# Dilated mixer: tokens sorted by class, half of one group's transposes on VectorE, operands at 256 bytes, seams' norms on VectorE

## The chip, the cores and the metric

The kernel runs on one core of a Trainium2 chip, as a single launch. The metric is the device time of that launch in microseconds (us), less is better. The engines are called as in the profile: PE is TensorE (matrix multiplies and transposes), PEld its weight loads, DVE is VectorE, ACT is ScalarE, POOL is GpSimd, SP is SyncE, which issues the weights' DMAs.

## The reference

A four-layer encoder works on 512 tokens of 1024 features, batch 1. Each layer is a mixer and a SwiGLU feed-forward part (F), each with a norm before and after and a residual. Layers 0 and 3 have the dilated mixer (A), layer 1 an axial-rope attention (B), layer 2 a latent attention (C). So the stages run A, F, B, F, C, F, A, F. The part that the change is mostly about is the dilated mixer:

```python
A_GROUPS = ((128, 1), (512, 4), (2048, 16))     # window, dilation
...
def mixer_a(x, wqkv, wo):
    qkv = (x @ wqkv).reshape(B, S, 3, A_NG, A_HEADS, A_HEAD_DIM)   # 3 groups, 16 heads of 64
    for g, (window, dilation) in enumerate(A_GROUPS):
        o, l = dilated_window_attention(qkv[:, :, 0, g], qkv[:, :, 1, g], qkv[:, :, 2, g], window, dilation, slopes[g])
    wgt = jax.nn.softmax(jnp.stack(lses, axis=0), axis=0)
    o = jnp.sum(wgt[..., None] * jnp.stack(outs, axis=0), axis=0)
    return o.reshape(B, S, -1) @ wo
```

In a group of dilation d a token attends to the tokens of its own residue mod d within the window, with a bias that is linear in the distance. With 512 tokens, the second group (d = 4) has four residues of 128 tokens each, and the third (d = 16) has sixteen of 32 tokens each.

## The kernel before, in words

**Numbers.** Everything is float32 in and out. A product is made from high and low parts: `split` (L136) rounds a tile to a high part on ACT (L138) and takes the rest on DVE (L139), and `mm3` (L170) issues three matmuls, high with high (L172), high with low (L173), low with high (L174). Weights arrive as `raw` by DMA from SP and are split to `whi`, `wlo`. The normed input of a stage is kept transposed in `yh`, `yl`, and the hidden values of a feed-forward part in `hT`. A trace row names out<-moving,stationary: `psa<-yh,whi` streams 512 columns of yh against a 128x128 block of whi, `psp<-whi,hT` streams whi against a block of hT.

**PSUM.** Banks of 128x512 float32 come in four tags with two buffers each: psa (projections), pss (scores), psp (transposes), pso (values).

**The dilated mixer** goes over eight pairs of heads p. A pair has eight units (hh, bp): hh is the head, bp 0 and 1 are the two halves of the first group's queries, bp 2 and 3 the two halves of the second and third group's. For bp 2 and 3 the 512 tokens stand in four blocks by residue mod 4; in a block's 128x256 tile of scores the columns 0 to 127 are the second group's keys and 128 to 255 the third group's, whose entries outside the residue mod 16 are put far away by the distance table `dist` (t2 in `const_tables`). Per unit: `scores` makes the matmuls, a DVE operation adds the bias and takes the row minimum (L625), ACT exponentiates (L628) into p; `transposes` turns p in four PE transposes 128x128 (L642) into one psp bank, split into pT (L138, L139); `values` multiplies pT with v. There are 64 units a mixer, two mixers in the program, so 128 units and 512 transposes at L642, of which 64 units have bp above 1. Between the units' steps the PE works at a filler, the projections of the next pair, in an order that is written out by hand; the other engines' order is made by a scheduler. At the end of a pair the group's maxima and sums go through HBM (`scr`) back into token order, by one DMA out (L632) and one in (L634), both issued by POOL, and `weigh` and `spread` make the weights of the groups from them. For the last pair `spread_fast` does that with transposes at L735.

**Seams.** At the end of a stage `rows_out` evacuates token tile t = 0 to 3 one after the other, adds to the residual h (L291), and makes the next stage's input with `pre_norm` (L191), whose transposes follow in `norm_t` (L226). `pre_norm` has two forms. The ordinary one multiplies h by the gain on POOL (L201, two operations of 128x512) while ACT sums the squares, and later scales one half on ACT (L209) and one on POOL (L210). The one called fast does both products in two DVE operations (L207) once the factor r is there (POOL, L218); only the first stage of the program uses it.

**Places in SBUF.** In the built program `yh` starts 192 bytes past a multiple of 256 in a partition, and so do `yl`, `raw`, `whi` and `wlo`; the pools of a stage (hT, pT, kd, y, q, kT, cT, wx, v) start 64 past one, and `ident` 128 past one.

Of the kernel before, what the change touches and what calls it, by code (L numbers as in the profile page):

```python
# [10 lines left out]
F32 = mybir.dt.float32  # L11
F32R = mybir.dt.float32r
AF = mybir.ActivationFunctionType
# [24 lines left out]
def const_tables():  # L38

    f = np.float32  # L40
    q = np.arange(P)[:, None]
    w = np.arange(2 * P)[None, :]
    d0 = np.abs(w - 64 - q)
    t0 = np.where(d0 <= 64, d0, BIG).astype(f)
    l = np.arange(P)[None, :]
    d1 = np.abs(l - q)
    t1 = np.where(d1 <= 64, 4.0 * d1, BIG).astype(f)
    t2 = np.where((l - q) % 4 == 0, 4.0 * d1, BIG).astype(f)
    dist = np.concatenate([t0, t1, t2], axis=1)

    def angles(pos, dim):
        half = dim // 2
        fr = np.power(f(10000.0), -np.arange(half, dtype=f) * f(2.0) / f(dim)).astype(f)
        return (pos.astype(f)[:, None] * fr[None, :]).astype(f)

    t = np.arange(S)
    cs, sn = [], []
    for pos in (t // 64, t % 64):
        a = angles(pos, 64)
        c, s = np.cos(a), np.sin(a)  # L60
        cs += [c, c]
        sn += [-s, s]
    bcos = np.concatenate(cs, axis=1).astype(f)
    bsin = np.concatenate(sn, axis=1).astype(f)

    a = angles(t, 32)
    c, s = np.cos(a).astype(f), np.sin(a).astype(f)
    ccos = np.concatenate([c, c], axis=1)
    csin = np.concatenate([-s, s], axis=1)
    sc = f(96.0 ** -0.5)  # L70
    cq = np.empty((P, S), f)
    cq[:64] = -sc
    cq[64:96] = -(ccos.T * sc)
    cq[96:] = -(csin.T * sc)
    return {
        "t_dist": dist,
        "t_bcos": bcos,
        "t_bsin": bsin,
        "t_ckr": np.concatenate([ccos, csin], axis=1),
        "t_cq": cq,  # L80
    }
# [26 lines left out]
class Net:  # L108
    def __init__(self, ctx, tc, a):
        self.tc, self.nc, self.a = tc, tc.nc, a  # L110
        nc = self.nc
        pool = lambda name, bufs, **k: ctx.enter_context(tc.tile_pool(name=name, bufs=bufs, **k))
        self.base = pool("base", 1)
        self.wp = pool("wp", 4)
        self.work = pool("work", 2)

        self.small = pool("small", 6)
        self.ps = pool("ps", 2, space=bass.MemoryType.PSUM)
        self.ident = self.base.tile([P, P], F32, name="ident")
        make_identity(nc, self.ident)  # L120
        self.mhalf = self.base.tile([P, 16], F32, name="mhalf")
        nc.vector.memset(self.mhalf, -0.5)
        self.h = [self.base.tile([P, D], F32, name=f"h{t}") for t in range(NB)]
        self.yh = self.base.tile([P, KD, S + 64], F32R, name="yh")
        self.yl = self.base.tile([P, KD, S + 64], F32R, name="yl")
        self.n = 0
# [120 lines left out]
    def rows_out(self, yp, stat, nf, w, acc_in, final, late=None, R=5):  # L247
# [98 lines left out]
        for t in range(NB):  # L346
            for pr in range(cut, npair):
                if pr == npair - 2 and t >= 2:
                    self.flush(1)
                for f in (2 * pr, 2 * pr + 1):  # L350
                    one(banks[t], f, t, ws[pr])
                yield 1.3
            evac(t, 1, banks[t])
            if "pre" not in gains:
                nc.sync.dma_start(out=self.a["out"][t * P:(t + 1) * P, :], in_=self.h[t])
            else:
                self.pending.append(lambda t=t, yn=self.pre_norm(t, gains["pre"]): self.norm_t(t, yn, final[2]))


    def ffn(self, i, final):  # L360
# [61 lines left out]


    def mixer_a(self, j, final):


        nc, tc = self.nc, self.tc
# [47 lines left out]
        def proj_v12(p):  # L475


            vt = {}

            def turn(g, tag="a"):  # L480
                bk = self.bank(tag)
                for c in range(NB):
                    nc.tensor.transpose(bk[:, c * P:(c + 1) * P], vt[g][:, c * P:(c + 1) * P], self.ident)
                if g == 1:
                    st["v12"] = [new(f"v12{i}", [P, NB, 256]) for i in range(2)]
                t = [x[:, :, (g - 1) * P:g * P] for x in st["v12"]]
                self.split(t[0], t[1], bk.rearrange("p (c e) -> p c e", c=NB))

            for g in (1, 2):
                wt = qk_load(g, 2, p)  # L490
                bk = self.bank("a")
                for k in range(KD):
                    qk_mm(bk, wt, slice(0, S), k)
                    yield 0.65
                    if g == 2 and k == 2:
                        turn(1)
                        yield 0.45
                vt[g] = self.work.tile([P, D], F32, tag="yn", name=self.uid("vt"))[:, :S]
                nc.scalar.activation(vt[g].rearrange("p (r l) -> p r l", r=NB),
                                     bk.rearrange("p (l r) -> p r l", r=NB), AF.Copy)  # L500
                if g == 1:
                    yield from wait(8 * p + 2)

            def rest(tag="a"):
                turn(2, tag)
                done.add(("v12", p))

            st["turn"] = rest
# [14 lines left out]

        lower, upper = slice(0, 64), slice(64, P)

        def lo_scaled(out, src, hi):
            nc.vector.scalar_tensor_tensor(out, src, -0.125, hi.bitcast(F32), op0=ALU.mult, op1=ALU.subtract)

        def qk_evac(bk, g, s):
            for hh in range(2):  # L530
                src = bk[hh * 64:hh * 64 + 64]
                if g == 0 and s == 0:
                    q = st["q", hh] = new(f"q{hh}", [P, S])
                    nc.scalar.activation(q[lower], src, AF.Copy, scale=-0.125)
                    lo_scaled(q[upper], src, q[lower])
                elif g == 0:
                    kh, kl = st["k", hh] = new(f"kh{hh}", [P, S]), new(f"kl{hh}", [P, S])
                    nc.scalar.activation(kh[lower], src, AF.Copy)
                    nc.scalar.activation(kh[upper], src, AF.Copy)
                    nc.vector.tensor_tensor(kl[lower], src, kh[lower].bitcast(F32), op=ALU.subtract)  # L540
                    nc.gpsimd.tensor_copy(kl[upper], kl[lower].bitcast(F32))
                else:
                    rows = (lower, upper)[g - 1]
                    src = src.rearrange("p (l r) -> p r l", r=4)
                    if s == 0:
                        if g == 1:
                            st["y", hh] = [new(f"y{hh}{i}", [P, S]) for i in range(2)]
                        h, l = [x[rows].rearrange("p (r l) -> p r l", r=4) for x in st["y", hh]]
                        nc.scalar.activation(h, src, AF.Copy, scale=-0.125)
                        lo_scaled(l, src, h)  # L550
                    else:
                        self.split(kd[hh][0][rows, :, g - 1, :], kd[hh][1][rows, :, g - 1, :], src)

        def proj_qk(p, g, s, unit):
            wt = qk_load(g, s, p)
# [30 lines left out]
        def scores(p, hh, bp):  # L586
# [42 lines left out]
            st["p", p, hh, bp] = pp  # L629
            if hh == 1 and bp == 3:  # L630
                sc = self.scr[p % 2]
                nc.gpsimd.dma_start(out=sc.rearrange("(l r) c -> l r c", r=4), in_=xs)  # L632
                xn = ap.tile([P, NB, 4], F32, tag="xn", name=self.uid("xn"), bufs=2)
                nc.gpsimd.dma_start(out=xn, in_=sc.rearrange("(b p) c -> p b c", p=P))  # L634
                st["xn", p] = xn

        def transposes(p, hh, bp):
            pp = st.pop(("p", p, hh, bp))
            tp = self.bank("p")
            for i in range(2):  # L640
                for c in range(2):
                    nc.tensor.transpose(tp[:, (2 * i + c) * P:(2 * i + c + 1) * P],  # L642
                                        pp[:, i, c * P:(c + 1) * P], self.ident)
            st["last"] = self.split(pT[0][:, bp % 2], pT[1][:, bp % 2], tp)

        def values(p, hh, bp):
# [33 lines left out]
            if bp == 3:  # L680
                if hh == 0:
                    st["op", p] = new("op", [P, S], F32)
                nc.scalar.activation(st["op", p][rows].rearrange("p (l r) -> p l r", r=4),
                                     out[:64].rearrange("p (r l) -> p l r", r=4), AF.Copy)

        def weigh(p):

# [601 lines left out]
    def run(self, stages):  # L1289
# [43 lines left out]
                self.rest(2)  # L1333
        for n, st in enumerate(stages):
            nxt = stages[n + 1] if n + 1 < len(stages) else None
            final = (post(st), pre(nxt) if nxt else None, bool(nxt) and nxt[0] == "A")
            kind, j, i = st
            run = {"F": self.ffn, "A": self.mixer_a, "B": self.mixer_b, "C": self.mixer_c}[kind]
            with ExitStack() as es:
# [39 lines left out]
```

## Time and profile before

| | |
|---|---|
| time, median of 3 runs | 3064.25 us (3064.14 to 3065.21) |
| profiled execution | 3065.5 us |
| its span | 3063.7 us |
| PE busy | 3026.5 us, 99% |
| PEld, DVE, ACT, POOL busy | 84%, 51%, 46%, 14% |
| mean granted clock of PE | 0.998 of full |

The span runs from the first instruction to the last of one profiled execution; its time has some 2 us around it. Busy is time in which an instruction of the engine was under way. Matmuls are pipelined, so each is recorded longer (389 ns for 512 columns) than the step from one start to the next. Full speed of the clock is 2.4 GHz.

### The profile page before, as it was taken

The numbers are of one execution on the slowest core, as the hardware profiler recorded it, in microseconds if no ns is written. First come the engines' busy times: TensorE is split into PE (matmuls) and PEld (weight loads), VectorE is DVE, ScalarE is ACT, GpSimd is POOL, SyncE is SP. The second block draws the span as 40 slices with busy tenths as digits, with TensorE's granted clock in tenths as the row PEclk, the third lists the DMA queues.
The fourth block names the chain that finished last, engine by engine and source line by source line (L and its number), as shares of the span: only waits on it lengthen the run. The fifth ranks groups of instructions, "written<-read, shape, count | busy, mean of one in ns | idle before, by whom it ended". The sixth has DMA issues, their size and how long they took to land.

```text
span 3063.7 us, 42230 instructions
## 1 busy us (share of the span) xinstructions
PE 3026.5 (99%) x16102; PEld 2568.6 (84%) x16102; DVE 1552.2 (51%) x3120; ACT 1420.5 (46%) x3073; POOL 430.3 (14%) x628
## 2 busy tenths in 40 slices
PE   9999999999999999999999999999999999999998
PEld 8888888888887888888888888888888888888886
DVE  5555556533346863333578633235555555643233
ACT  5555556532234653223478632234555555542232
POOL 1111111300003330000254400003011111210000
PEclk9999999999999999999999999999999999999999
DMA  5222222332332123333211233332322223233332
GB/s 148 76 84 77 83 84 84 108 100 95 97 108 67 56 83 97 100 93 105 75 51 36 90 96 97 96 101 75 90 83 84 79 82 90 84 101 99 91 99 73
DMA packets 286810, 269.11 MB, mean 88 GB/s; under 512 B 9776, under 2 KB 246544, under 8 KB 286608
## 3 DMA queue, kind: packets, MB, share of 16 engines
q1 hardware_dynamic: 280736, 250.84, 27.3%
q0 software_dynamic: 5872, 15.59, 1.8%
q8 instruction: 126, 2.06, 0.3%
q14 instruction: 76, 0.62, 0.1%
HBM read 264.04 MB, written 2.34 MB: 87 GB/s over the span
## 4 chain that ended last, share of the span: by engine, by line
PE 61%; DVE 2%; ACT 1%; POOL 1%; issue 0%; DVEq 0%; POOLq 0%; ACTq 0%
PE psa L174 8%; PE psa L172 8%; PE psa L173 8%; PE pss L172 4%; PE pss L173 4%; PE pss L174 4%; PE pso L173 3%; PE pso L174 3%; PE pso L172 3%; PE psp L174 3%; PE psp L173 3%; PE psp L172 3%; PE psp L873 1%; PE psp L642 1%; DVE wlo L139 1%; PE pso L897 0%
## 5 line engine op out<-in xcount | busy, mean ns | idle before, releaser
L139 DVE TENSOR_TENSOR wlo<-raw,whi 128x512 fp32r<-128x512 f32 (+1 forms) x895 | 592.3, 702 | 776.2 <-ACT whi L138 774.4
L138 ACT ACTIVATE whi<-raw 128x512 fp32r<-128x512 f32 (+2 forms) x928 | 524.6, 613 | 651.4 <-PE pss L173 140.8
L172 PE MATMUL psa<-yh,whi 128*128 128x512 f32 (+1 forms) x1408 | 550.3, 391 | 0.2 <-ACT yh L138 0.2
L173 PE MATMUL psa<-yl,whi 128*128 128x512 f32 (+1 forms) x1408 | 536.5, 381 | 6.9 <-DVE yl L139 6.9
L174 PE MATMUL psa<-yh,wlo 128*128 128x512 f32 (+1 forms) x1408 | 537.1, 381 | 0.0
L174 PEld LDWEIGHTS psa<-yh,wlo 128*128 128x128 f32 x1408 | 264.7, 188 | 52.9
L173 PEld LDWEIGHTS psa<-yl,whi 128*128 128x128 f32 x1408 | 265.7, 189 | 49.1 <-DVE yl L139 9.1
L172 PEld LDWEIGHTS psa<-yh,whi 128*128 128x128 f32 x1408 | 265.4, 188 | 40.5 <-ACT yh L138 0.5
L218 POOL TENSOR_TENSOR r<-v,mhalf 128x1 f32<-128x1 f32 x64 | 38.7, 605 | 1492.3 <-DVE v L216 1490.5
L172 PE MATMUL pss<-yh,whi 128*128 128x512 f32 (+1 forms) x448 | 160.9, 359 | 0.0
L173 PE MATMUL pss<-yl,whi 128*128 128x512 f32 (+1 forms) x448 | 160.7, 359 | 0.0
L174 PE MATMUL pss<-yh,wlo 128*128 128x512 f32 (+1 forms) x448 | 160.7, 359 | 0.0
L139 DVE TENSOR_TENSOR pT<-psp,pT 128x512 fp32r<-128x512 f32 x128 | 88.3, 690 | 123.0 <-ACT pT L138 122.0
L138 ACT ACTIVATE hT<-sg 128x512 fp32r<-128x512 f32 x88 | 55.0, 625 | 198.5 <-DVE sg L406 198.5
L172 PE MATMUL pso<-yh,whi 128*128 128x512 f32 (+1 forms) x384 | 143.2, 373 | 0.0
L174 PE MATMUL pso<-yh,wlo 128*128 128x512 f32 (+1 forms) x384 | 142.6, 371 | 0.0
L172 PE MATMUL psp<-yh,whi 128*128 128x512 f32 (+1 forms) x384 | 142.6, 371 | 0.0
L173 PE MATMUL psp<-yl,whi 128*128 128x512 f32 (+1 forms) x384 | 142.6, 371 | 0.0
L174 PE MATMUL psp<-yh,wlo 128*128 128x512 f32 (+1 forms) x384 | 142.6, 371 | 0.0
L173 PE MATMUL pso<-yl,whi 128*128 128x512 f32 (+1 forms) x384 | 142.6, 371 | 0.0
L172 PE MATMUL psa<-whi,yh 128*128 128x256 f32 (+3 forms) x412 | 135.0, 328 | 2.8 <-ACT junk L984 2.0
L174 PE MATMUL psa<-whi,yl 128*128 128x256 f32 (+3 forms) x412 | 132.5, 322 | 1.0 <-DVE yl L139 0.9
(425 smaller groups left out, 6616.4 us busy)
## 6 DMA issues: line engine op xcount, KB each, us to landing
raw<-a_wqkv SPq DMA_DIRECT2D x144, 512.0 KB, 3.8
raw<-ffn_wg SPq DMA_DIRECT2D x88, 512.0 KB, 3.8
raw<-ffn_wu SPq DMA_DIRECT2D x88, 512.0 KB, 3.8
raw<-ffn_wd SPq DMA_DIRECT2D x88, 512.0 KB, 3.8
raw<-a_wo SPq DMA_DIRECT2D x16, 512.0 KB, 3.8
wb<-scw POOLq DMA_DIRECT2D x28, 256.0 KB, 4.3
raw<-b_wqkv SPq DMA_DIRECT2D x12, 512.0 KB, 3.7
raw<-b_wo SPq DMA_DIRECT2D x8, 512.0 KB, 4.5
```

Of the source, the lines that this page charges most:

```text
L138: x = nc.scalar.activation(hi, src, AF.Copy)
L139: y = (eng or nc.vector).tensor_tensor(lo, src, hi.bitcast(F32), op=ALU.subtract)
L172: nc.tensor.matmul(out, sh, mh, start=start, stop=False)
L173: nc.tensor.matmul(out, sh, ml, start=False, stop=False)
L174: nc.tensor.matmul(out, sl, mh, start=False, stop=stop)
L218: nc.gpsimd.tensor_tensor(r, v, self.mhalf[:, 0:1], op=ALU.pow)
L642: nc.tensor.transpose(tp[:, (2 * i + c) * P:(2 * i + c + 1) * P], pp[:, i, c * P:(c + 1) * P], self.ident)
L873: nc.tensor.transpose(tp[:, c * P:(c + 1) * P], x[:, c * P:(c + 1) * P], self.ident)
```

## The change

It has three parts.

**Sorted tokens and transposes on DVE.** In the blocks of the second and third group, place i now holds token l = 4 (i mod 32) + i div 32 of the residue, so that the tokens of one residue mod 16 stand together in a run of 32; `by16` and `blocks` are the views that do this wherever q, k, v, and the output are copied, and the distance tables are sorted alike. The third group's 128x128 probabilities are then zero outside four 32x32 squares on the diagonal. DVE has a transpose that turns each 32x32 square of a tile in its place; for bp above 1 it now turns the third group's two 128x128 tiles (c = 1), straight into the psp bank, beside the two PE transposes of the second group. Two things follow from the views: the low part of y is made in four DVE operations of 64x128 instead of one of 64x512, and the DMA to `scr` becomes four DMAs of 32 partitions.

**Operands at 256 bytes.** The pool `small` has 5 instead of 6 buffers a tag, a tile `pad` is put in, and `mhalf` is twice as wide. With that yh, yl, raw, whi, wlo and the stages' pools start at a multiple of 256 bytes; `ident` stays.

**Seams' norms.** `pre_norm` takes its fast form for the tiles t = 2 and 3 where the next stage is A or F.

```diff
-    l = np.arange(P)[None, :]
-    d1 = np.abs(l - q)
+    i = np.arange(P)
+    l = 4 * (i % 32) + i // 32
+    dl = l[None, :] - l[:, None]
+    d1 = np.abs(dl)
...
-    t2 = np.where((l - q) % 4 == 0, 4.0 * d1, BIG).astype(f)
+    t2 = np.where(dl % 4 == 0, 4.0 * d1, BIG).astype(f)
...
-        self.small = pool("small", 6)
+        self.small = pool("small", 5)
+        pool("pad", 1).tile([P, 56], F32, name="pad")
...
-        self.mhalf = self.base.tile([P, 16], F32, name="mhalf")
+        self.mhalf = self.base.tile([P, 32], F32, name="mhalf")
...
-                self.pending.append(lambda t=t, yn=self.pre_norm(t, gains["pre"]): self.norm_t(t, yn, final[2]))
+                self.pending.append(lambda t=t, yn=self.pre_norm(t, gains["pre"], t > 1 and final[3]): self.norm_t(t, yn, final[2]))
...
+        by16 = lambda x: x.rearrange("p (l c r) -> p r c l", c=4, r=NB)
+        blocks = lambda x: x.rearrange("p (r c l) -> p r c l", r=NB, c=4)
...
-                        h, l = [x[rows].rearrange("p (r l) -> p r l", r=4) for x in st["y", hh]]
+                        h, l = [blocks(x[rows]) for x in st["y", hh]]
                         nc.scalar.activation(h, src, AF.Copy, scale=-0.125)
-                        lo_scaled(l, src, h)
+                        for r in range(NB):
+                            lo_scaled(l[:, r], src[:, r], h[:, r])
...
-                nc.gpsimd.dma_start(out=sc.rearrange("(l r) c -> l r c", r=4), in_=xs)
+                for c in range(4):
+                    nc.gpsimd.dma_start(out=sc.rearrange("(l c r) x -> c l r x", c=4, r=NB)[c],
+                                        in_=xs[32 * c:32 * c + 32])
...
-                    nc.tensor.transpose(tp[:, (2 * i + c) * P:(2 * i + c + 1) * P],
-                                        pp[:, i, c * P:(c + 1) * P], self.ident)
+                    (nc.vector if bp > 1 and c else nc.tensor).transpose(
+                        tp[:, (2 * i + c) * P:(2 * i + c + 1) * P], pp[:, i, c * P:(c + 1) * P],
+                        *([] if bp > 1 and c else [self.ident]))
...
-            final = (post(st), pre(nxt) if nxt else None, bool(nxt) and nxt[0] == "A")
+            final = (post(st), pre(nxt) if nxt else None, bool(nxt) and nxt[0] == "A", bool(nxt) and nxt[0] in "AF")
```

How the instructions move is read from the order in which each engine issues them. On PE, at the first unit with bp above 1 (pair 0, head 0), the order before has four transposes of the same p into the bank psp_143 in a row, and only the first waits, for PE's own earlier work:

```order
L174 MATMUL psa_138_946<-yh_81,wlo_137_940 128x512
L642 MATMUL psp_143_1001<-ident_70,p_132_921 128x128 [waits PE_49]
L642 MATMUL psp_143_1001<-ident_70,p_132_921 128x128 x3
L172 MATMUL psa_151_1028<-yh_81,whi_149_1021 128x512 [waits DVE_49,PE_49]
L173 MATMUL psa_151_1028<-yl_82,whi_149_1021 128x512
```

The changed kernel has two at the same place (its line numbers are some 11 higher here, L653 for L642), and the second waits for DVE:

```order
L177 MATMUL psa_138_962<-yh_85,wlo_137_956 128x512
L653 MATMUL psp_143_1017<-ident_74,p_132_937 128x128 [waits PE_49]
L653 MATMUL psp_143_1017<-ident_74,p_132_937 128x128 [waits DVE_49]
L175 MATMUL psa_151_1044<-yh_85,whi_149_1037 128x512 [waits PE_49]
L176 MATMUL psa_151_1044<-yl_86,whi_149_1037 128x512
```

Two of the four PE transposes are gone, and between the two that are left stands a wait for DVE, with the next projection behind it. The rest of PE's order is the same, row for row. On DVE, at the same unit, the transposes into psp_143 are new, each waits for PE, and a weight's split stands between them; the split of the finished bank into pT follows some rows later:

```order
L679 TENSOR_TENSOR ot_128_905<-pso_142_1000,ot_128_905 64x512 [waits Activation_49]
L653 STREAM_TRANSPOSE psp_143_1017<-p_132_937 128x128 [waits DVE_49,PE_49]
L142 TENSOR_TENSOR wlo_185_1285<-raw_183_1283,whi_184_1284 128x512 [waits DMAHW5_49,Activation_49]
L653 STREAM_TRANSPOSE psp_143_1017<-p_132_937 128x128 [waits PE_49]
L142 TENSOR_TENSOR wlo_185_1285<-raw_183_1283,whi_184_1284 128x512 [waits Activation_49]
L548 TENSOR_TENSOR kl0_145_1025<-psa_138_962,kh0_144_1024 64x512 [waits Activation_49]
```

So the first DVE transpose comes after the first PE transpose, the second PE transpose after the first of DVE, and the second of DVE after the second of PE: the two engines take turns on the bank. On DVE at the seam from the first dilated mixer to its feed-forward part, the order before runs from the residual of tile 2 to the low parts yl of tile 1, and on to the next weight:

```order
L291 SCALAR_TENSOR_TENSOR h2_79<-y_848_5688,r1_901_5884,h2_79 128x512 x2
L139 TENSOR_TENSOR wlo_935_5995<-raw_933_5993,whi_934_5994 128x512 x2
L203 TENSOR_SCALAR v0_907_5897<-ss_903_5889 128x1
L139 TENSOR_TENSOR yl_82<-psp_910_5917,yh_81 128x4x128
L139 TENSOR_TENSOR yl_82<-pso_911_5924,yh_81 128x4x128
L216 SCALAR_TENSOR_TENSOR v1_908_5899<-ss_905_5893,v0_907_5897 128x1
L139 TENSOR_TENSOR wlo_938_6051<-raw_936_6049,whi_937_6050 128x512 x2
```

In the changed kernel the two products of tile 2 stand behind the low parts, between the halves of the next weight's split:

```order
L294 SCALAR_TENSOR_TENSOR h2_83<-y_848_5812,r1_901_6008,h2_83 128x512 x2
L142 TENSOR_TENSOR wlo_935_6115<-raw_933_6113,whi_934_6114 128x512 x2
L206 TENSOR_SCALAR v0_907_6019<-ss_903_6013 128x1
L142 TENSOR_TENSOR yl_86<-psp_910_6039,yh_85 128x4x128
L142 TENSOR_TENSOR yl_86<-pso_911_6046,yh_85 128x4x128
L219 SCALAR_TENSOR_TENSOR v1_908_6021<-ss_905_6016,v0_907_6019 128x1
L142 TENSOR_TENSOR wlo_938_6171<-raw_936_6169,whi_937_6170 128x512
L210 SCALAR_TENSOR_TENSOR yn_902_6012<-h2_83,r1_909_6023,gain_839_5784 128x512 x2
L142 TENSOR_TENSOR wlo_938_6171<-raw_936_6169,whi_937_6170 128x512
```

Ahead of yl nothing moved on DVE; what is gone is POOL's pair of products for tiles 2 and 3 (L201).

## Rows read from the trace of the kernel before

**Rows 1.** The page's part 1: busy time, share of the span, instructions.
```profile
PE 3026.5 (99%) x16102; PEld 2568.6 (84%) x16102; DVE 1552.2 (51%) x3120; ACT 1420.5 (46%) x3073; POOL 430.3 (14%) x628
```

**Rows 2.** Waits on PE, whole span: total us, times, longest.
```profile
PE psa L173 <- DVE yl L139: 6.9, 8, 1.3
...
PE pso L173 <- DVE pT L139: 1.8, 3, 0.7
```

**Rows 3.** Stretch of the first dilated mixer: busy us and count, clock, DMA.
```profile
40.00:575.00 535.00, 532.64 (x3177) 458.61 (x3176) 308.44 (x714) 304.94 (x694) 78.56 (x144) 1.00 0.30 85
```

**Rows 4.** Timeline of PE at a unit's transposes: start, us, instruction.
```profile
93.16 0.60 PE L642 MATMUL psp<-ident,p 128*128 128x128 f32 x4
...
93.83 0.40 PE L173 MATMUL psa<-yl,whi 128*128 128x512 f32 x1
```

**Rows 5.** PE by line and form: count, busy us, mean ns, idle before.
```profile
L642 PE MATMUL psp<-ident,p 128*128 128x128 f32 x512 | 76.7, 272 | 0.0
```

**Rows 6.** DVE by line and form.
```profile
L139 DVE TENSOR_TENSOR pT<-psp,pT 128x512 fp32r<-128x512 f32 x128 | 88.3, 690 | 123.0 <-ACT pT L138 122.0
...
L994 DVE TENSOR_TENSOR xs<-xn,tab 128x128 f32<-128x128 f32 x32 | 7.2, 284 | 0.2
...
L203 DVE TENSOR_SCALAR v<-ss 128x1 f32<-128x1 f32 x32 | 4.9, 152 | 9.1 <-ACT junk L199 9.1
```

**Rows 7.** Timelines of PE and DVE where DVE waits for a PE score.
```profile
135.72 0.28 PE L611 MATMUL pss<-kl,q 128*128 128x192 f32 x1
...
136.03 0.42 DVE L625 CUSTOM_DVE_ANT_0 p<-pss,bias 128x256 f32<-128x256 f32 x1 [0.26 <-PE pss L611]
```

**Rows 8.** Timeline where values wait for the split of pT.
```profile
96.39 0.22 PE L172 MATMUL pso<-pT,v 128*64 128x128 f32 x1
...
96.62 0.67 DVE L139 TENSOR_TENSOR pT<-psp,pT 128x512 fp32r<-128x512 f32 x1
...
97.34 0.27 PE L173 MATMUL pso<-pT,v 128*64 128x128 f32 x1 [0.73 <-DVE pT L139]
```

**Rows 9.** Timelines of DVE, POOL and PE at the first mixer's seam.
```profile
578.54 3.49 DVE L139 TENSOR_TENSOR wlo<-raw,whi 128x512 fp32r<-128x512 f32 x2
...
582.01 0.67 DVE L139 TENSOR_TENSOR yl<-psp,yh 128x512 fp32r<-128x512 f32 x1
...
578.19 3.29 POOL L201 TENSOR_TENSOR yn<-h,gain 128x512 f32<-128x512 f32 x2 [1.02 <-PE psp L226]
...
582.74 0.39 PE L173 MATMUL psa<-yl,whi 128*128 128x256 f32 x1 [1.32 <-DVE yl L139]
```

**Rows 10.** Timelines of POOL and PE at the seam into the second mixer.
```profile
2128.01 4.42 POOL L776 MEMSET kd<- 64x512 f32 x8
...
2118.85 0.39 PE L173 MATMUL psa<-yl,whi 128*128 128x256 f32 x1 [0.67 <-DVE yl L139]
...
2133.29 0.66 PE L226 MATMUL pso<-ident,yn 128*128 128x128 f32 x4 [1.49 <-POOL yn L210]
```

**Rows 11.** PE by line and form: matmuls of 512 columns.
```profile
L172 PE MATMUL psp<-yh,whi 128*128 128x512 f32 x320 | 124.5, 389 | 0.0
...
L172 PE MATMUL psp<-whi,hT 128*128 128x512 f32 x144 | 57.1, 396 | 0.0
...
L172 PE MATMUL psp<-wx,hT 128*128 128x512 f32 x32 | 12.5, 390 | 0.0
```

**Rows 12.** Timeline of PE in a feed-forward part: first and last of 68 matmuls.
```profile
659.64 0.39 PE L174 MATMUL pss<-yh,wlo 128*128 128x512 f32 x1
...
674.83 0.39 PE L172 MATMUL psa<-yh,whi 128*128 128x512 f32 x1
```

**Rows 13.** POOL by line; timelines of DVE and PE at the mixer's end.
```profile
L632 POOL DMA_DIRECT2D scr<-xs x16 | 10.2, 640 | 26.7 <-ACT p L628 25.5 <-issue 1.3
...
546.58 0.43 DVE L731 COPY p<-dd 128x512 f32<-128x512 f32 x1
...
550.04 1.03 PE L735 MATMUL psp<-ident,p 128*128 128x128 f32 x8
```

More of the change, by code (lines that the diff above doesn't have):

```diff
@@ L498, in proj_v12 @@
                 vt[g] = self.work.tile([P, D], F32, tag="yn", name=self.uid("vt"))[:, :S]
-                nc.scalar.activation(vt[g].rearrange("p (r l) -> p r l", r=NB),
-                                     bk.rearrange("p (l r) -> p r l", r=NB), AF.Copy)
+                nc.scalar.activation(blocks(vt[g]), by16(bk), AF.Copy)
                 if g == 1:
@@ L543, in qk_evac @@
                     rows = (lower, upper)[g - 1]
-                    src = src.rearrange("p (l r) -> p r l", r=4)
+                    src = by16(src)
                     if s == 0:
@@ L547, in qk_evac @@
                             st["y", hh] = [new(f"y{hh}{i}", [P, S]) for i in range(2)]
-                        h, l = [x[rows].rearrange("p (r l) -> p r l", r=4) for x in st["y", hh]]
+                        h, l = [blocks(x[rows]) for x in st["y", hh]]
                         nc.scalar.activation(h, src, AF.Copy, scale=-0.125)
-                        lo_scaled(l, src, h)
+                        for r in range(NB):
+                            lo_scaled(l[:, r], src[:, r], h[:, r])
                     else:
-                        self.split(kd[hh][0][rows, :, g - 1, :], kd[hh][1][rows, :, g - 1, :], src)
+                        self.split(*[x[rows, :, g - 1, :].rearrange("p r (c l) -> p r c l", c=4) for x in kd[hh]], src)
         def proj_qk(p, g, s, unit):
@@ L682, in values @@
                     st["op", p] = new("op", [P, S], F32)
-                nc.scalar.activation(st["op", p][rows].rearrange("p (l r) -> p l r", r=4),
-                                     out[:64].rearrange("p (r l) -> p l r", r=4), AF.Copy)
+                nc.scalar.activation(st["op", p][rows].rearrange("p (l c r) -> p l c r", c=4, r=NB),
+                                     out[:64].rearrange("p (r c l) -> p l c r", r=NB, c=4), AF.Copy)
         def weigh(p):
```

## The prediction

> **What bounds the kernel now.** The page's busy row comes first: PE is at work for 3026.5 us of the span, the others for about half or less [rows 1]. Then the waits on PE: the largest names 6.9 us over eight times (DVE's low parts yl, at seams), the split of pT stands for 1.8 us in three [rows 2]. So the time is PE's instructions, one after another, and an edit pays or costs by what it does to PE's steps from start to start. The stretch of the first dilated mixer shows the same with the numbers that matter there: PE 532.64 of 535 us, DVE 308.44 us (58%) in 714 instructions, so 0.43 us each, POOL 15% [rows 3].
>
> **Transposes in turns.** Before, a unit's four transposes begin at 93.16 and the second matmul behind them at 93.83 [rows 4]; with 0.23 us for the one matmul between (68 starts from 659.64 to 674.83, so 226.7 ns a step [rows 12]) the four take 0.44 us. They are 512 in all [rows 5], 64 units of four lose two each: if nothing else happened, 128 x 0.11 = 14 us of PE would be saved.
> But the order shows the two engines taking turns. From the start of PE's first transpose: 0.27 until it ends [rows 5], 0.03 until DVE starts (135.72 + 0.28 to 136.03 [rows 7]), the DVE transpose, 0.05 until PE starts again (96.62 + 0.67 to 97.34 [rows 8]). PE's second transpose takes a step of 0.11 plus 0.05 for a start from rest (0.27 beside 0.22 us in the same rows), and only then the projection behind it runs. A DVE transpose of 128x128 is nowhere in the trace. The nearest row is a DVE operation of 128x128 with 284 ns [rows 6]; below it cannot come under an operation on one column, 152 ns, and above I take one on 512 columns, 690 ns [rows 6]. I choose 0.28, the same count of elements. Then a unit takes 0.27 + 0.03 + 0.28 + 0.05 + 0.16 = 0.79 against 0.44: **+0.35 us**, times 64 = +22 us.
> DVE may also be busy when PE's first transpose ends. It is so 58% of the time, with half of a 0.43 us operation left on average: 0.125 us, times 64 = +8 us; bounds 0 and 0.35 (always half of a split of 0.69). Together **+30 us**, from +14 (0.15, no queue: 0.22 a unit) to +71 (0.69 and 0.35: 1.11 a unit).
> A rule speaks against this step too. The Trainium skill, "PSUM — Partial Sum Buffer", section "PSUM bank collisions raise a hardware error", says that two engines must not touch one bank in the same partitions at the same time, even in different columns, and that one should guard by bank and not by address. The order agrees, with a wait at each turn; no run here shows two engines in one bank at once. Without that rule nothing would keep the DVE transposes from running beside those of PE, and by such a sum this term would be -14 and not +30.
>
> **pT comes later.** The split of the bank now starts after the second DVE transpose, one hand-over and one DVE operation behind PE's second, so some 0.7 us after where it was when no split of a weight lies between the DVE transposes, 1.4 when one does. Most units have more room than that; the first with bp 2 in a pair has none (PE waits 0.73 at 97.34 [rows 8], three such waits in all [rows 2]). Half of the delay is taken up where PE itself was held by the turns. With 16 such units in the two mixers and some 0.15 us each: **+2.5 us**, bounds 0 and 15 (one more us at each).
>
> **Other work that is added.** The low part of y as four operations instead of one: 4 x 0.28 against 0.69 on DVE [rows 6], +0.45, sixty times, 27 us of DVE; with the transposes (128 x 0.28 = 36 us) DVE rises to some 64% of the mixers. No wait on PE names y; its cover is the rest of the pair's projections. I take 0 on the path beyond the queue term. Three more DMA issues a pair at 0.64 us [rows 13] put 1.9 us onto POOL's queue, ahead of the DMA that brings the sums back, and of the next bias. Only the last pair has no later work between: there the weights are copied at 546.58 to 547.01 and PE takes them up at 550.04 without a wait, 3.0 us later [rows 13]. Hidden: 0, at most +1 twice if the four DMAs also land later.
>
> **Seams.** At the first mixer's seam two splits of a weight take 3.49 us where two of 0.69 are usual, while POOL multiplies 128x512 tiles for 3.29 us; yl comes behind them on DVE, and PE waits 1.32 us for it [rows 9]. The change takes POOL's products of tiles 2 and 3 away, so yl is some 2 us earlier and the wait is gone. Three more seams (into the other feed-forward parts that follow A, B and C) read like it, longest 1.3 each [rows 2]: 5.1 us. The Trainium skill, "SBUF — State Buffer", tells of a port that DVE and GpSimd share and that one locks against the other; the two rows of 3.49 and 3.29 us side by side agree. At the seam into the second mixer yl costs 0.67, and the transposes of tile 3 wait 1.49 because POOL sets eight tiles of kd for 4.42 us ahead of the scaling [rows 10]; that scaling goes to DVE. Sum 7.3 us, and each wait also costs the matmul behind it a start from rest (0.1). What is late next is yn of tiles 2 and 3, two DVE operations behind POOL's factor, needed some 8 us after; at the second mixer's seam a low part now stands behind them, some 0.4 us. **-8 us**, from -8.5 to 0.
>
> **Operands at 256 bytes.** Before, the weights' tiles lie 192 past a multiple of 256, hT 64 past. A matmul whose stream and next block differ in that phase takes 396 ns in the down projection, where streams with equal phases take 389 (yh by whi, both 192) and 390 (wx by hT, both 64) [rows 11]. Six rows of 144 and six of 176 are like the 396 one (means 394 to 396): 1920 matmuls x 4 to 6 ns = 8 to 11 us, and some 470 of the other mixers 2 to 3. After it all phases are equal. **-11 us**, from -14.5 to 0 (if hT is slow for another reason).
>
> **Sum.** +30 + 2.5 - 8 - 11 = +13.5, say +14. The profiled execution took 3065.5 us (a span of 3063.7 and 1.8 around it), which the sum would take to 3079; it stands 1.25 above the median of 3064.25, to which I add: **3078 us**. The bounds all at once: +14 - 8.5 - 14.5 = -9, and +71 + 15 + 2 = +88.
>
> **The rivals.**
> Likeliest (0.45): turns as above, 3070 to 3094.
> *The turns are dearer* (0.12): a DVE transpose at 0.69 adds 0.41 x 64 = 26, so 3104; with pT late at its bound 3117. For it: DVE is fuller after than before; against it: operations of this size take 0.28.
> *The turns are cheap* (0.16): a DVE transpose near 0.15 and DVE free at the turns give +14 in place of +30, so 3062, no change.
> *The streams gain too* (0.27), the case on the other side. Every step of 512 columns takes 226.7 ns [rows 12], 13.4 more than 512 / 2.4 = 213.3 at the granted clock of 1.00 (2.4 GHz). If the place of an operand, and not only the phase between two, is part of these 13 ns, some 13,800 matmuls (16,102 less 1,272 transposes and about 1,000 with a block of 64 columns) become shorter. It decides from 1.5 ns each: 13,800 x 1.5 = 20 takes 3078 to 3058. At 11 ns it is 150 us, about 2927. For it: nothing else in the trace explains the 13 ns; against it: equal phases at 64 and at 192 are within 1 ns of each other [rows 11], as if the place alone did nothing. The Trainium skill, "TensorE: Matmul & The Clock Gate", section "Back-to-back issue gap", gives N / 2.4 + 2.5 ns for a step, 215.8 at 512 columns; the row's 226.7 is above that, and this rule taken as what an aligned stream reaches is this rival's far end.
> That the alignment does nothing at all is inside the first case: 3089.
>
> **How the numbers follow.** The time is that of the first case, 3078. A measurement of this kernel tells about 0.2%, 6 us, from no change: below 3058 is faster, above 3070 slower. Faster is the rival of the streams and a little of the cheap turns, 0.29; same is most of the cheap turns, 0.14; slower 0.57. For 8 in 10 the range goes from 3038, which takes in the streams' gain up to 3 ns and leaves out some 0.13, to 3110, which leaves out some 0.05.
>
> **What would show it.** In the profile after: the second transpose of a unit with a wait for DVE of 0.3 to 0.5 us, 64 times, as the first or second row of PE's waits, about 25 to 35 us; the DVE transpose near 0.28 us; the mixers' stretches some 16 us longer each; no wait for yl above 1 us at the four seams, and splits near 0.69 there; the down projection at 389 to 391 ns. It is wrong if streams of yh fall below 389 ns (the rival of the streams), if DVE's transpose is 0.15 or 0.7, or if PE waits for pT at many units.

## The result and the profile after

The changed kernel takes 3088.12 us (median of 4 runs, 3085.92 to 3091.68), the one before 3064.28 in the same comparison. The ratio is 1.0078, with a 95% interval of 1.0061 to 1.0096, so it is slower by some 24 us. The forecast was 3078, with 3038 to 3110 as its range.

The page's busy row of the changed kernel answers to [rows 1]:

```profile
PE 3018.9 (98%) x15974; PEld 2556.1 (83%) x15974; DVE 1612.6 (52%) x3460; ACT 1415.0 (46%) x3063; POOL 412.6 (13%) x646
```

PE does 128 instructions and 7.6 us less, in a span that is 24 us longer. So the time went into waits. The largest waits on PE, against [rows 2] (line numbers are 3 higher at the splits and the matmuls, 11 at the transposes):

```profile
PE psp L653 <- DVE psp L653: 40.0, 64, 3.0
PE pso L176 <- DVE pT L142: 4.5, 10, 0.5
...
PE psa L176 <- DVE yl L142: 1.7, 5, 0.6
```

The first row did not exist before: in each of the 64 units with bp above 1, PE's second transpose waits for the DVE transpose, 40.0 us in all. The wait for yl at the seams fell from 6.9 us to 1.7. The wait for pT rose from 1.8 to 4.5.

The two dilated mixers carry the loss. The first matmul behind the first mixer starts at 602.09 us where it was 581.15, so 20.9 us later; the second mixer runs from 2122.41 to 2717.22, 594.8 us, where it was 567.8 (2117.91 to 2685.73). That is +21 and +27, where some 16 each were forecast.

The timeline of one unit, first PE and then DVE, shows a turn, against [rows 4]:

```profile
92.89 0.27 PE L653 MATMUL psp<-ident,p 128*128 128x128 f32 x1
93.58 0.33 PE L653 MATMUL psp<-ident,p 128*128 128x128 f32 x1 [0.42 <-DVE psp L653]
93.66 0.48 PE L175 MATMUL psa<-yh,whi 128*128 128x512 f32 x1
93.98 0.39 PE L176 MATMUL psa<-yl,whi 128*128 128x512 f32 x1
```

```profile
93.19 0.33 DVE L653 STREAM_TRANSPOSE psp<-p 128x128 f32<-128x128 f32 x1
93.55 0.69 DVE L142 TENSOR_TENSOR wlo<-raw,whi 128x512 fp32r<-128x512 f32 x1
94.16 0.32 DVE L653 STREAM_TRANSPOSE psp<-p 128x128 f32<-128x128 f32 x1
```

PE's first transpose ends at 93.16, DVE starts at 93.19 and ends at 93.52, PE starts again at 93.58, 0.69 us after its first start. The matmuls of the projection stand behind that wait. From the first transpose to the second matmul behind them it is 1.09 us (92.89 to 93.98) where it was 0.67.

Of the 64 units 44 wait these 0.42 us and twelve up to 0.66. The other eight wait 1.03 to 3.02 us, because DVE is not free when its turn comes. At 226.99 PE makes its first transpose; the DVE rows of that place:

```profile
226.35 2.22 DVE L142 TENSOR_TENSOR wlo<-raw,whi 128x512 fp32r<-128x512 f32 x2 [1.40 <-ACT whi L141]
228.49 0.31 DVE L653 STREAM_TRANSPOSE psp<-p 128x128 f32<-128x128 f32 x1
```

and of PE and POOL:

```profile
228.86 0.33 PE L653 MATMUL psp<-ident,p 128*128 128x128 f32 x1 [1.60 <-DVE psp L653]
```

```profile
225.92 1.30 POOL L755 TENSOR_TENSOR op<-op,wb 128x512 f32<-128x512 f32 x1 [5.18 <-DMA wb<-scw]
```

Two splits of a weight stand ahead of the transpose on DVE. They wait for ACT first, and beside POOL's product the two take 2.22 us, where two take 1.29 at the seam below; PE waits 1.60 us for what takes DVE 0.31. If every turn cost the 0.42 of the plain ones, the 64 would make 27 us; the other 13 us of the 40.0 are such queues, 11.5 of them in the eight units.

At the first mixer's seam, against [rows 9], the two splits take 1.29 us and PE goes on without a wait (DVE, then PE):

```profile
599.49 1.29 DVE L142 TENSOR_TENSOR wlo<-raw,whi 128x512 fp32r<-128x512 f32 x2
...
600.96 0.69 DVE L142 TENSOR_TENSOR yl<-psp,yh 128x512 fp32r<-128x512 f32 x1
```

```profile
602.09 0.28 PE L175 MATMUL psa<-yh,whi 128*128 128x256 f32 x1
602.20 0.28 PE L176 MATMUL psa<-yl,whi 128*128 128x256 f32 x1
```

And the rows by line and form that answer to [rows 6] and [rows 11]:

```profile
L653 DVE STREAM_TRANSPOSE psp<-p 128x128 f32<-128x128 f32 x128 | 41.0, 321 | 68.3 <-PE psp L653 67.9
```

```profile
L175 PE MATMUL psp<-yh,whi 128*128 128x512 f32 x320 | 124.5, 389 | 0.0
...
L175 PE MATMUL psp<-whi,hT 128*128 128x512 f32 x144 | 56.3, 391 | 0.0
...
L175 PE MATMUL psp<-wx,hT 128*128 128x512 f32 x32 | 12.4, 389 | 0.0
```

A DVE transpose takes 321 ns. The streams against hT went from 396 to 391 ns, those of yh stayed at 389.

### The profile page after: what moved, and what is told of

The parts are those of the page before. It is cut to its first block, busy times and chain, and to the rows that moved or that the text cites. A ratio compares the mean times of both kernels' runs of the same rounds, so it can differ in the third digit from the quotient of the medians.

```text
span 3087.9 us, 42321 instructions
## 1 busy us (share of the span) xinstructions
PE 3018.9 (98%) x15974; PEld 2556.1 (83%) x15974; DVE 1612.6 (52%) x3460; ACT 1415.0 (46%) x3063; POOL 412.6 (13%) x646
## 5 line engine op out<-in xcount | busy, mean ns | idle before, releaser
L141 ACT ACTIVATE pT<-psp 128x512 fp32r<-128x512 f32 x128 | 76.5, 597 | 141.8 <-DVE psp L653 77.5
```

What stands on the lines that cost most here:

```text
L141: x = nc.scalar.activation(hi, src, AF.Copy)
```

## The experiments

Each kernel is timed against runs of the kernel before on the same chip (medians 3064.5 to 3065.4 us); ratios are to these, with a 95% interval in brackets. An interval reaches some 3 to 4 us to either side. Where two experiments are compared, their medians are, and a difference of a few us between two of them is not told from none.

**The parts one by one.** The first experiment undoes only the transposes on DVE; everything else of the change stays.

```diff
-                    (nc.vector if bp > 1 and c else nc.tensor).transpose(
-                        tp[:, (2 * i + c) * P:(2 * i + c + 1) * P], pp[:, i, c * P:(c + 1) * P],
-                        *([] if bp > 1 and c else [self.ident]))
+                    nc.tensor.transpose(tp[:, (2 * i + c) * P:(2 * i + c + 1) * P],
+                                        pp[:, i, c * P:(c + 1) * P], self.ident)
```

> The changed kernel with all four transposes of a unit back on TensorE; sorted tokens, four low parts of y, four DMAs, operands at 256 bytes and the seams' norms stay. Theory (the turns on the bank are the whole loss, 40.0 us of waits for DVE on PE and some 8 us around them): 3044 us, 3040 to 3048, and PE waits for DVE's transposes not at all. Rival (the sorted views, the four low parts and the four DMAs cost part of the 48 us that the two mixers became longer): 3052 or more.

Measured: 3049.13 us, ratio 0.9949 (0.9937 to 0.9962). PE has no wait for a transpose any more; the first row of its waits is

```profile
PE pso L176 <- DVE pT L142: 3.7, 8, 0.7
```

It lies just outside the theory's range, short of the rival: 39.0 us go with the DVE transposes, more than the whole difference between after and before, since the other parts gain. In the profiled executions the two mixers are 17.8 and 21.5 us shorter than in the changed kernel, which is these 39 us. Of the 48 us that they had become longer, 9 stay.

The second does that part alone on the kernel before: `small`, `mhalf`, the pad and `pre_norm` as before, sorted tokens and DVE transposes as in the change.

```diff
-        self.small = pool("small", 5)
-        pool("pad", 1).tile([P, 56], F32, name="pad")
+        self.small = pool("small", 6)
...
-        self.mhalf = self.base.tile([P, 32], F32, name="mhalf")
+        self.mhalf = self.base.tile([P, 16], F32, name="mhalf")
...
-... self.pre_norm(t, gains["pre"], t > 1 and final[3]) ...
+... self.pre_norm(t, gains["pre"]) ...
```

> The kernel before with the sorted tokens and the transposes on DVE alone: no operands at 256 bytes, seams' norms as before. Theory (the parts add up: the mixers' 48 us stand alone): 3112 us, 3108 to 3116. Rival (part of the mixers' loss comes with the new places of operands or from the seams): 3105 or less.

Measured: 3105.67 us, ratio 1.0133 (1.0119 to 1.0147), 41 us slower than before. The expected 3112 was a miss: the 48 us were read from one pair of executions of before and after. The changed kernel's was 1.6 above its median, which is only part of the 6 us; the rest stays open. That the parts add up holds within the intervals: +41.1, with the -9.6 and -7.0 that the next two show, makes +24.5, and +23.8 was measured. The waits on PE:

```profile
PE psp L652 <- DVE psp L652: 37.8, 64, 3.3
PE psa L175 <- DVE yl L141: 6.9, 8, 1.3
PE pso L175 <- DVE pT L141: 4.9, 10, 0.6
```

The turns cost about the same without the other two parts, and yl is as late as it was before.

The third has the operands at 256 bytes alone, the fourth the seams' norms alone.

```diff
-        self.small = pool("small", 6)
+        self.small = pool("small", 5)
+        pool("pad", 1).tile([P, 56], F32, name="pad")
...
-        self.mhalf = self.base.tile([P, 16], F32, name="mhalf")
+        self.mhalf = self.base.tile([P, 32], F32, name="mhalf")
```

> The kernel before with the operands at 256 bytes alone. Theory (phase between stream and block is all that counts): the rows of hT by whi go from 394-396 to 389-391 ns, the time to 3054 us, 3051 to 3057. Rival (the gain seen in the changed kernel's feed-forward parts comes from elsewhere): 3061 or more.

Measured: 3054.92 us, ratio 0.997 (0.9959 to 0.9981). The rows by line and form of PE:

```profile
L173 PE MATMUL psp<-yh,whi 128*128 128x512 f32 x320 | 124.5, 389 | 0.0
...
L173 PE MATMUL psp<-whi,hT 128*128 128x512 f32 x144 | 56.3, 391 | 0.0
...
L173 PE MATMUL psp<-wx,hT 128*128 128x512 f32 x32 | 12.4, 389 | 0.0
```

yh and its weights moved from 192 past a multiple of 256 bytes to 0, and the mean of their stream stayed at 389 ns; hT, which had stood in another phase than the weights, gained 5. The twelve rows of whi and wlo by hT take 747.6 us together where they took 758.1, so they hold the whole gain. That the phase is the cause, and not the place of hT, is not quite shown: no run changes the one without the other, and the other five rows of wx by hT, with equal phase before and after, went from between 390 and 392 to 389.

```diff
-... self.pre_norm(t, gains["pre"]) ...
+... self.pre_norm(t, gains["pre"], t > 1 and final[3]) ...
...
-... bool(nxt) and nxt[0] == "A")
+... bool(nxt) and nxt[0] == "A", bool(nxt) and nxt[0] in "AF")
```

> The kernel before with the seams' norms on VectorE alone. Theory (the waits for yl at four seams and at the one into the second mixer go, 7 us): 3057 us, 3055 to 3059, and no wait of PE for yl above 0.7 us. Rival (another operation is late in their place): 3061 or more.

Measured: 3057.56 us, ratio 0.9979 (0.997 to 0.9988). Waits on PE:

```profile
PE psa L173 <- DVE yl L139: 1.4, 4, 0.6
```

The waits for yl over 0.7 us are gone, and no new wait stands in their place. Both parts together, without sorted tokens (the two diffs above on one kernel):

> The kernel before with the operands at 256 bytes and the seams' norms, without sorted tokens. Theory (the two add up, -9.6 and -7.0): 3048 us, 3046 to 3050. Rival (one takes part of what the other gives): 3052 or more. Beside the kernel with all transposes on PE (3049) it tells what the sorted views, the four low parts and the four DMAs cost: about 1 us if the parts add up.

Measured: 3047.67 us, ratio 0.9944 (0.993 to 0.9958). That is 17.7 below its own runs of the kernel before, where the two alone make 16.6: they add up within the intervals. The first experiment, which has the sorted tokens as well, is 1.5 us above this, less than the two intervals tell apart: the views, the four low parts of y and the four DMAs are hidden, or nearly so. One place in the two profiles is not: in the last pair of the second mixer PE waits 2.26 us for yl (at 2630.07), and 0.65 without the sorted tokens (2625.54). There the second of the two DMAs that bring the weights of the groups into SBUF (`wb`) is issued behind the first one's end, at 2624.11 after 2620.74, where without the sorted tokens the two follow each other at once at 2617.82. Whether the four DMAs are the reason, no run shows.

**The turns.** The first of these exchanges two loops, so that the same four transposes are issued PE, PE, DVE, DVE, still into one bank.

```diff
-            for i in range(2):
-                for c in range(2):
+            for c in range(2):
+                for i in range(2):
                     (nc.vector if bp > 1 and c else nc.tensor).transpose(
```

> The changed kernel with the loops over i and c exchanged, so that a unit issues its two PE transposes first and its two DVE transposes after them, into the same bank; the work is the same. Theory (the loss is PE standing still in the middle of the turns, not the DVE transposes as such): no wait of PE for DVE's transposes, PE saves 14 us against four transposes, pT comes some 0.4 us later at 16 tight units: 3037 us, 3032 to 3046. Rival (DVE work and a late pT are the loss): 3060 or more, with the waits moved to the split of pT.

Measured: 3062.46 us (3059.09 to 3067.45), ratio 0.9993 (0.9984 to 1.0002), which cannot be told from the kernel before. The waits:

```profile
PE pso L176 <- DVE pT L142: 13.3, 16, 1.1
PE pso L175 <- ACT pT L141: 8.1, 6, 1.5
```

No wait for a transpose is left, and 25.7 us of the loss went with it. But 3037 was a miss, and the rival named most of the reason: pT now waits for PE's two transposes and then for two of DVE, behind whatever DVE has in its queue, and 21.4 us of waits stand at 22 places where it was 3.7 with all transposes on PE. They are units with little room, in head 0 of the pairs and in the last pair.

These 17.7 us more are not all. PE saves 14 us against the kernel with all transposes on PE, and the run is 13.3 above it, so 27 have to be found. The rest agrees with TensorE's clock: its mean is 0.994 to 0.997 in the eleven runs, with the slowest at 0.994 and the fastest at 0.997, and 0.998 to 0.999 in the runs with all transposes on PE. The medians, 0.996 and 0.999, differ by 0.003 of 3050 us, which is 9 us by estimate. In the profile the clock falls behind the waits for pT. At 226.37 and 227.71 PE has waited 1.26 and 1.06 us, and from 228 to 231 the granted clock is 0.52, so 1.2 GHz for nearly all of it (busy us of each engine, granted clock, DMA):

```profile
228.00:231.00 3.00, 3.00 (x16) 2.61 (x15) 0.95 (x2) 0.00 (x0) 0.00 (x0) 0.52 0.03 5
```

The next doubles the disputed cost: the first DVE transpose of each unit is issued twice, to the same place.

```diff
                 for c in range(2):
-                    (nc.vector if bp > 1 and c else nc.tensor).transpose(
+                    for _ in range(2 if bp > 1 and c and not i else 1):
+                        (nc.vector if bp > 1 and c else nc.tensor).transpose(
...
```

> The changed kernel with the first DVE transpose of each of the 64 units issued twice, into the same place. Theory (PE waits for it in each unit, so its duration of 0.32 us counts in full, and a weight's split of 0.69 stands between the two in some units): 20 to 45 us more than the changed kernel, 3108 to 3133. Rival (PE waits for a queue on DVE that has room, not for the transpose): under 10 us more.

Measured: 3115.77 us, 27.7 above the changed kernel, ratio to before 1.0166 (1.0152 to 1.018). PE's waits:

```profile
PE psp L654 <- DVE psp L654: 70.9, 64, 2.9
```

They grew by 30.9 us in 64 places, 0.48 each: the transpose of 0.32 and, in some units, a split between the two. The plain wait is 0.78 us in 37 units, where it was 0.42 in 44. PE pays for what DVE does in its turn in full.

Two more use DVE only where pT has room, 34 of the 64 units, once with PE's transposes first (the diff) and once in the changed kernel's order (the same without the exchange of the loops).

```diff
+            roomy = bp > 1 and p < 7 and (hh or (bp == 3 and p % 2))
-            for i in range(2):
-                for c in range(2):
-                    (nc.vector if bp > 1 and c else nc.tensor).transpose(
+            for c in range(2):
+                for i in range(2):
+                    (nc.vector if roomy and c else nc.tensor).transpose(
...
```

> The changed kernel with PE's transposes first as in the run with the loops exchanged, and the DVE transposes only in the 34 units in which pT has room (head 1 of pairs 0 to 6, and bp 3 of head 0 in pairs 1, 3 and 5, of both mixers); the other units have four PE transposes. Theory (a DVE transpose pays where no turn is taken and pT has room: 34 x 0.22 us below the kernel with all transposes on PE, 3049): 3042 us, 3039 to 3045, waits for pT about 4 us in all. Rival (the DVE work itself costs, by the splits that come later behind it): 3048 or more.

Measured: 3043.11 us, ratio 0.9928 (0.9916 to 0.994), 6.0 below the kernel with all transposes on PE; 34 x 0.22 = 7.5 was expected. The wait for pT is as it was there, so the DVE work as such costs little or nothing:

```profile
PE pso L176 <- DVE pT L142: 3.7, 8, 0.7
```

> The run with DVE transposes in the 34 roomy units, but in the order of the changed kernel, so that the engines take turns there. Theory (a turn costs PE 0.58 us between its two transposes and 0.05 for the start from rest, whether pT has room or not): 34 x 0.63 = 21 us above the run in the other order, 3063 us, 3058 to 3070, with 34 waits of PE for DVE's transposes. Rival (the changed kernel lost by pT in the tight units, not by turns as such): under 10 us above it.

Measured: 3066.43 us, ratio 1.0003 (0.9994 to 1.0012), 23.3 above the run in the other order, with the same units and the same work. The waits:

```profile
PE psp L654 <- DVE psp L654: 15.7, 34, 0.7
PE pso L176 <- DVE pT L142: 4.0, 8, 0.7
```

pT is no later. The turn costs 0.69 us a unit (23.3 / 34), of which 0.46 is the wait that the profile shows; the rest is that PE's first transpose runs to its end (0.27 us in place of a step of 0.11) and the second starts from rest (0.05), 0.21 together.

**A place of its own.** The last one lets DVE write its two transposes into a tile in SBUF (the buffer `junk`, which the mixer does not use) and splits pT in two halves. PE's two transposes have the bank to themselves. Units with bp 0 and 1 keep their four PE transposes.

```diff
...
+            t3 = self.work.tile([P, 512], F32, tag="junk", name=self.uid("junk"), bufs=1)[:, :2 * P].rearrange("p (i q) -> p i q", i=2)
+            for i in range(2):
+                nc.vector.transpose(t3[:, i], pp[:, i, P:])
+                nc.tensor.transpose(tp[:, i * P:(i + 1) * P], pp[:, i, :P], self.ident)
+            h, l = [x[:, bp % 2].rearrange("p (i c q) -> p i c q", i=2, c=2) for x in pT]
+            self.split(h[:, :, 1], l[:, :, 1], t3)
+            st["last"] = self.split(h[:, :, 0], l[:, :, 0], tp[:, :2 * P].rearrange("p (i q) -> p i q", i=2))
```

> The changed kernel with the DVE transposes of all 64 units written into a tile in SBUF and not into the bank that PE writes; each unit's split into pT is done in two halves, one from that tile and one from the bank. Theory (what cost 40 us was the shared bank; with a place of its own a DVE transpose waits only for p, and PE keeps the 14 us): 3038 us, 3034 to 3046, no wait of PE for a DVE transpose, waits for pT under 10 us. Rival (a second split on ACT and DVE makes pT late as in the run with PE's transposes first, 21 us of waits): 3055 or more.

Measured: 3040.67 us (3039.55 to 3040.91), ratio 0.992 (0.9906 to 0.9933), the lowest median of all and 25 us below its own runs of the kernel before (3065.41); the run with the 34 roomy units, 3043.11, is not told from it. DVE by line and form, and the largest wait on PE:

```profile
L660 DVE STREAM_TRANSPOSE junk<-p 128x128 f32<-128x128 f32 x128 | 35.2, 297 | 5.1 <-ACT p L637 4.0
...
L142 DVE TENSOR_TENSOR pT<-junk,pT 128x256 fp32r<-128x256 f32 x64 | 30.1, 471 | 27.4 <-ACT pT L141 27.4
...
L142 DVE TENSOR_TENSOR pT<-psp,pT 128x256 fp32r<-128x256 f32 x64 | 26.7, 418 | 15.5 <-ACT pT L141 13.8
```

```profile
PE pso L176 <- DVE pT L142: 7.8, 12, 0.9
```

DVE's transposes are no longer tied to PE (5.1 us of idle time ahead of them, 68.3 before), and they run as soon as p is there. PE keeps 8.5 us of the 14 that its 128 transposes took (3049.13 to 3040.67); 4.1 us of the difference is pT, from 3.7 to 7.8. The run changes the place of DVE's result and splits pT in halves; which of the two brings the wait for pT down from the 21.4 us of the exchanged loops, it doesn't tell.

## Why the prediction was right, and where its sizes were off

**Transposes in turns: right, somewhat too small.** The mechanism was read from the order, and the profile shows it step by step: PE, DVE, PE, DVE, with the projection behind PE's second. The forecast was +30 for the turns and 2.5 for a late pT, 32.5 together; the first experiment gives 39.0. The rows add up to about that: 40.0 us of waits, and 64 times the 0.21 of a first transpose that runs to its end and a second that starts from rest, 13.4, less the 14 saved, make 39.4. A DVE transpose took 0.32 us where 0.28 was chosen, and the hand-over back 0.06 instead of 0.05, so PE's two starts are 0.69 apart and not 0.63: 4 us. The queue on DVE was put at 0.125 us a unit, 8 us; it is 13, because it is not spread evenly: eight units stand behind stretched splits or operations that wait themselves, and the average of a busy share doesn't see that.

**pT comes later: the number is near, the cause only in part.** The wait is 4.5 against 1.8 us, +2.7 where 2.5 was said. But with all four transposes on PE it is 3.7 already, and with the operands at 256 bytes alone 3.4, so beside that kernel the DVE transposes add 0.8. With the sorted tokens and the DVE transposes alone it is 4.9, 3.1 above the kernel before. These are single executions, and the two don't agree on what the term is; that it came to 2.7 is in part luck. The experiment with the loops exchanged shows what was hidden by the turns: as soon as PE does not stand still, the same chain of transposes, ACT and DVE is late by 21 us in all.

**Other work that is added: right within the noise.** The kernels with and without the sorted views, four low parts and four DMAs differ by 1.5 us, which the intervals don't tell from the 0 that was said; the bound was twice 1 us, should the DMAs land later, and the one longer wait above, 2.26 in place of 0.65, is at such a place.

**Seams: right.** -7.0 alone, where -8 was said; the waits of [rows 9] and [rows 10] are what went, 5.2 of the 6.9 us for yl and the one for the scaling. Two splits next to each other take 1.29 us instead of 3.49 at the first mixer's seam, in the run with the seams' norms alone too. POOL's products are what that run takes away beside them, so they were the cause, as the row suggested.

**Operands at 256 bytes: right.** -9.6 alone, where -11 was said, and it is the rows of hT that gain, 396 to 391 in the one shown. The reading that equal phases at 64 and 192 are within 1 ns took the lowest of the six rows of wx by hT, 390; the others stand at 390 to 392.

**The rivals.** That the streams gain too is refuted: in the third experiment the streams of yh, whose place changed and whose phase did not, kept their 389 ns. The place does nothing there, 192 or 0. The 13 ns over 213 that a step has stay unexplained. That the turns are cheap is refuted too, by a transpose of 0.32 us and not 0.15, by the 40.0 us of waits, and by the doubled transpose. That they are dearer by a transpose of 0.69 did not come; what the turns cost above the forecast is more the queue than the transpose.

**The sum.** +39.0 - 7.0 - 9.6 + 1.5 = +23.9, and +23.8 was measured; the forecast was +14. The turns with pT were 6.5 too small, the two gains together 2.4 too large, and 1.5 was taken as nothing. The 39.0 and the 1.5 are themselves differences to and from the first experiment, so what the sum tests is only that the two gains add up. The time lies nearer to the 3089 that was given for an alignment that does nothing than to 3078; that is chance, since the third experiment shows the gain.

The program follows a rule that the Trainium skill gives in "PSUM — Partial Sum Buffer", section "PSUM bank collisions raise a hardware error": a bank is to be guarded between engines. These runs show the price here, against the kernel with all transposes on PE: 39.0 us with the bank shared in turns, and -8.5 us with a place of its own. No run had two engines in a bank at once, so what happens then is not shown here.

What stays open: how much of the 4.1 us of a late pT in the last experiment could be had by leaving the tight units to PE was not tried, nor another order on DVE for the eight units with a queue.

## What to carry to other kernels

When work is moved from the engine that is always busy to one that is idle, look at where its result lands: if both engines write one PSUM bank by turns, the busy engine waits out the idle one's work and its queue, and can lose more than it gave away, here 39 us after the 14 saved are taken off. Issue the busy engine's part in one piece, which alone was not enough here, or give the other its own tile. Then look for whoever consumes the result with the least room, since there the moved work comes too late even when no turn is taken.

## What the runs showed of the hardware that was not expected

A DVE transpose of 128x128 float32 takes 321 ns on average into PSUM and 297 into SBUF, in the order of an elementwise operation of that size (284, [rows 6]).

At the seam from the first feed-forward part into stage B, which the change does not touch, the changed kernel gains some 2 us by estimate, 0.5 of a wait and six matmuls of 0.23. PE waits there for ACT, 2.0 us before and 1.5 after. The stretches behind that wait, before and then after (busy us of each engine, granted clock, DMA):

```profile
966.00:970.00 4.00, 4.00 (x13) 3.12 (x12) 3.77 (x15) 0.00 (x0) 0.86 (x1) 0.59 0.00 0
```

```profile
981.00:985.00 4.00, 4.00 (x19) 3.27 (x18) 3.80 (x14) 0.00 (x0) 0.85 (x1) 1.00 0.00 0
```

Before, the granted clock is 0.59 in these 4 us, so for most of them at 1.2 GHz, and PE does 13 matmuls; after it is 1.00 (2.4 GHz) and 19. The run with the seams' norms alone, with a wait of 2.0 as before, has 0.69 at that place, the one with the operands alone, with a wait of 1.9, has 1.00 behind it. Why the one falls and the other doesn't is not settled by these runs.

The clock takes back more than that elsewhere, some 5 us by estimate from the three stretches here. In the profile of the changed kernel it is 0.57 from 2669 to 2673, behind the wait of 3.02 us for a DVE transpose (2668.16), 0.57 from 2338 to 2342 behind one of 1.95 (2337.70), and 0.50 from 2608 to 2611 behind one of 1.88 (2606.99). Two of its four runs have a mean of 0.999 and take 3085.92 and 3086.55 us; the other two, at 0.997 and 0.996, take 3089.69 and 3091.68. The forecast had no term for this.
